# Score maxima in runs of three groups, and an output projection in two dense stretches

## The chip, the cores and the metric

The kernel runs on one core of a Trainium2 chip. The time is in device microseconds (us): the median of three runs of the whole kernel. Five engines work beside each other, each through its own list of instructions in order, and wait for each other by semaphores: TensorE (PE: matmuls; PEld is its weight load), VectorE (DVE), ScalarE (ACT), GpSimd (POOL), and SyncE (SP), which starts the DMA transfers. PE writes into PSUM, eight banks of 128 partitions x 512 float32 numbers. DVE and ACT read PSUM; in this kernel POOL works on SBUF only.

## The reference

One encoder layer over 4096 tokens and 16 meta tokens of width 1024. Per token it is (cut to what matters):

```python
u = rmsnorm(h, norm_g)
f_in, f_gate, q, k, v, a_gate = split(u @ w_in)
f_out = fourier_branch(f_in, w_fmix, b_fmix) * silu(f_gate)     # 512 columns
q, k = rope(rmsnorm(q, q_g)), rope(rmsnorm(k, k_g))             # 8 q heads, 2 kv heads, dim 64
p = softmax(q @ k.T * 64 ** -0.5)                               # over all 4112 keys
a_out = (p @ v) * silu(a_gate)                                  # 512 columns
h = h + concat(f_out, a_out) @ w_out                            # output projection
return rmsnorm(h, final_g)[:, 16:]
```

## The kernel before

Phase A projects the tokens and writes q, k, v and the gates to DRAM. Phase B, which the change is in, does the Fourier branch, the attention, the output projection and the last norm. The Fourier work is finished within the first four pairs; what follows after them is attention with an output projection beside it.

Attention goes in 32 *pairs* `i` = (query block `b` of 512 queries, `p` of four pairs of heads). A pair has 66 *steps* `j`: two heads, 33 tiles of 128 keys each. In a step, PE multiplies one key tile with 512 queries (two matmuls, L1101 and L1102, into a score bank `s`: QK below), ACT takes the exponential (L1105, `pe`), DVE or POOL subtracts its bfloat16 half to get a float16 rest `rr` (L1107; the set `on_dve` says which steps go to DVE), and PE multiplies both with the values into the accumulator `o` (nine small matmuls: PV below). PV runs five steps behind QK (`LAG`).

A softmax needs the maximum of each query's scores. It is found one pair ahead: 32 *groups* a pair (4 query tiles x 8 chunks of 512 keys). A group is two matmuls of 64 rows (L1032), one for each head, which sit in the two halves of the PE array and run beside each other, into the two banks of a tile `m`, and then a DVE reduce of 1024 numbers a partition (L1034). The list `AT` has 16 steps, after whose QK two groups are done. I call such a place a *window*. At the end of the pair `red` (j 61), `fin` (63) and `put` (64) turn the maxima into a row of `qB` for the next pair.

From pair 4 on, pair `i` also does the output projection of one 128-token tile of the block before (`out_units`, L1197): 48 matmuls of 512 columns, 24 for each half of the 1024 output columns, into the one bank `po`. They stand one a step, at steps 15 to 38 and 39 to 62; at the end of each half DVE adds the residual (`hh`, L1202). `mf_parts` and `out_tr` split the Fourier and attention parts of that tile into two float16 halves, which a DMA transposes. The norm of the tile (`out_end`) follows in the next pair at the steps of `NORM`: one square of 1024 columns on ACT (L1214), a few tiny DVE instructions, and a scaling (L1228).

PSUM before: two tiles `m` of two banks (pool `pm`), two score banks (`pq`), `o` and `po`. Nothing but the order of the Python code sets the order on each engine: `top.enter_context(tc.manual_schedule())`. Buffers of a pool are taken in turn, and an instruction that writes one waits for the last reader of what was in it. After pair 31 a tail projects the last block.

Of the kernel before, what the change touches and what calls it, by code (L numbers as in the profile page):

```python
# [738 lines left out]

def phase_b(tc, a, pool, mm3, id32, id16, sc):  # L740
# [10 lines left out]
    with ExitStack() as st:  # L751
# [5 lines left out]
        pm = pool(st, "pm", 2, PSUM)  # L757
        pq = pool(st, "pq", 2, PSUM)
        pv = pool(st, "pv", 1, PSUM)
        pp = pool(st, "po", 1, PSUM)  # L760
# [66 lines left out]
        def dft_units(i, spare):  # L827
# [12 lines left out]
            def one(x, slot, chunk, w, first, last):  # L840
                if not ps:
                    ps.append((pv if spare else pp).tile([P, 512], F32, tag="o" if spare else "po", name="pd"))
# [37 lines left out]
        def trans(u, early):  # L880
            n, sk = (64, stk8) if seq[u] is LAST else (P, stk)
            if early:
                ps = pq.tile([P, 512], F32, tag="s", name="s").rearrange("p (g c)->p g c", c=P)
            else:
                ps = pm.tile([P, 2, 512], F32, tag="m", name="m")[:, 0].rearrange("p (g c)->p g c", c=P)
# [40 lines left out]
        def mix(u, early):  # L926
            n = 64 if seq[u] is LAST else P
            mo = mos[:, 2 * (u % 2):2 * (u % 2) + 2]
            if early:
                t = [pq.tile([P, 512], F32, tag="s", name="s") for _ in range(2)]  # L930
# [92 lines left out]
        def max_units(i):  # L1023
# [4 lines left out]
            def grp(s, c):  # L1028
                t = pm.tile([P, 2, 512], F32, tag="m", name="m")
                for e in range(2):  # L1030
                    rs = slice(64 * e, 64 * e + 64)
                    T.matmul(t[:, e], q[rs, p, s * P:(s + 1) * P], K[kv][rs, 0, c * 512:(c + 1) * 512],  # L1032
                             start=True, stop=True)
                V.tensor_reduce(mx[:, s, :, c], t, axis=AX.X, op=ALU.max)  # L1034

            def meta():
# [4 lines left out]
                t = pm.tile([P, 2, 512], F32, tag="m", name="m")  # L1041
# [19 lines left out]
            def fin():  # L1061

                t = pm.tile([P, 2, 512], F32, tag="m", name="m")
                T.matmul(t[:, 0, :P], n, id16, start=True, stop=True)
                rowt.append(t)
# [11 lines left out]
            return [(lambda s=s, c=c: grp(s, c)) for s, c in order], [meta] if first else [], red, fin, put  # L1077
# [18 lines left out]
        def step(h, kv, t, qa, qb, acc, ob, gate):  # L1096
            d = {}

            def qk(eng):
                s = pq.tile([P, 512], F32, tag="s", name="s")  # L1100
# [49 lines left out]
        def mf_parts(b, s):  # L1150
            mf = mfs.pop((b, s))
            hl = ld["sh1"].tile([P, 2, 512], F16, tag="mh", name="hl")

            def high():
                S.activation(hl[:, 0], mf, AF.Copy)

            def low():
                V.tensor_tensor(out=hl[:, 1], in0=mf, in1=hl[:, 0], op=ALU.subtract)

            def turn():  # L1160
                mt = w1.tile([P, 8, P], F16, tag="mt", name="mt")
                dma_t(mt, hl.rearrange("p w c->p (w c)"))
                mts[b, s] = [mt]

            def turn_last():
                dma_t(hv[:, 8 * s:8 * s + 4], hl[:, 0])
                dma_t(lv[:, 8 * s:8 * s + 4], hl[:, 1])

            return high, low, turn_last if b + 1 == NQB else turn

# [4 lines left out]
        def out_tr(b, s):  # L1175
            src = obs[b][:, s]
            hl = ld["sh1"].tile([P, 2, 512], F16, tag="ml", name="ah")
            S.activation(hl[:, 0], src, AF.Copy)

            def low():  # L1180
                V.tensor_tensor(out=hl[:, 1], in0=src, in1=hl[:, 0], op=ALU.subtract)
                at = w1.tile([P, 8, P], F16, tag="at", name="at")
                dma_t(at, hl.rearrange("p w c->p (w c)"))
                mts[b, s].append(at)

            return low

        def out_units(b, s):
# [3 lines left out]
            def one(k, j):  # L1192
                if j == 0:
                    d["po"] = pp.tile([P, 512], F32, tag="po", name="po")
                cs = slice(k * 512, (k + 1) * 512)
                i, w = j // 3, j % 3
                T.matmul(d["po"], mts[b, s][i // 4][:, i % 4 + (4 if w == 2 else 0)],  # L1197
# [9 lines left out]
        def out_end(b, s, d):  # L1207

            xr, hh = pst.pop((b, s)), d["hh"]
            ss = sm.tile([P, 1], F32, tag="ss", name="ss")  # L1210
            rf = sm.tile([P, 1], F32, tag="rf", name="rf")

            def square():
                S.activation(xr, hh, AF.Square, accum_out=ss)  # L1214

            t = sm.tile([P, 1], F32, tag="r1t", name="r1t")
            h = sm.tile([P, 1], F32, tag="r1h", name="r1h")

            def guess():
                V.tensor_scalar(out=ss, in0=ss, scalar1=1.0 / D, scalar2=EPS, op0=ALU.mult, op1=ALU.add)  # L1220
                root0(rf, ss, t, h)
# [4 lines left out]
            def scale():  # L1226
                yo = w1.tile([P, D], F32, tag="yo", name="yo")
                V.scalar_tensor_tensor(out=yo, in0=hh, scalar=rf, in1=fgb[0], op0=ALU.mult, op1=ALU.mult)  # L1228
                t0 = b * QB + s * P
                dma(a["out"][t0:t0 + P], yo)  # L1230

            return square, guess, newton, newton, newton, scale
# [18 lines left out]
        MT, TR, O0, O1 = 60, 12, 15, 39  # L1251
        NORM = [9, 13, 17, 21, 28, 32]
# [4 lines left out]
        gs += meta  # L1257
        n = 0
        INIT = 11
        while gs:  # L1260
            gs.pop(0)()
            catch_up()
            if gs:
                gs.pop(0)()
# [37 lines left out]
        prev = None  # L1302
        for i, (b, p) in enumerate(pairs):
            if p == 1 and b + 1 < NQB:
                qload(b + 1)
            if i > 4:
                load_xr(b - 1, p)
            elif i == 4:
                load_mf(0, 0)
            ready = {}  # L1310
# [265 lines left out]
```

## Time and profile before

| | |
|---|---|
| median of 3 runs | 3201.99 us (3200.11 to 3205.67) |
| profiled execution | 3203.48 us, its span 3201.7 us, granted PE clock 0.995 |
| busy over the span | PE 98 %, DVE 74 %, POOL 72 %, ACT 52 % |
| 1500 to 2500 us, of 100 us | DVE 79.4 to 81.9, POOL 76.8 to 83.0, ACT 56.0 to 59.7 |
| pairs 4 to 30 | 27 pairs, 72.7 to 73.4 us each |

Busy PE says little here: the record of a 512-column matmul is 379 ns long, and the next one starts 215 ns after it. What PE really does is read from starts: how far one step's first QK matmul lies behind that of the step before. The timeline gives them.

### The profile page before, as it was taken

Reading aid. Unit: us, or ns where it says so; the run is one execution under the profiler, and the core shown is the slowest. Engines: PE = TensorE matmul, PEld = TensorE weight load, DVE = VectorE, ACT = ScalarE, POOL = GpSimd, SP = SyncE. Lnnn points to the kernel's source line nnn. Section 1 sums busy time; section 2 is a strip of 40 time slices with the busy share of each in tenths; the row PEclk is TensorE's granted clock in tenths of the full one; section 3 lists DMA queues with packets and bytes.
Section 4 is the critical chain, followed back from the end, with each engine's and each line's share of the span. In section 5 each row is a group of like instructions: output and inputs, shape, how many; then the busy total and the mean of one; then the engine's idle time right before and its main releaser. Section 6 shows DMA issues by size and latency. Waiting matters only on the chain.

```text
span 3201.7 us, 77151 instructions
## 1 busy us (share of the span) xinstructions
PE 3146.1 (98%) x32291; PEld 1831.4 (57%) x32291; DVE 2373.2 (74%) x3241; ACT 1667.2 (52%) x2965; POOL 2304.3 (72%) x2174
## 2 busy tenths in 40 slices
PE   8999999998999999999999999999999999999998
PEld 4555555545666655555555555555555555555554
DVE  6666566647677778878888778788887887788774
ACT  5433333324555555555555555555555555555563
POOL 5655565536777788877877888887787778888762
PEclk9999999999999999999999999999999999999999
DMA  7444544648422221012111211201120111111112
GB/s 243 146 161 147 152 156 153 182 155 228 131 68 86 78 61 31 28 28 64 28 28 38 54 28 31 58 28 28 38 54 28 35 41 43 31 31 28 28 49 68
DMA packets 238832, 247.67 MB, mean 77 GB/s; under 512 B 134658, under 2 KB 182658, under 8 KB 235538
## 3 DMA queue, kind: packets, MB, share of 16 engines
q1 hardware_dynamic: 224658, 217.57, 23.6%
q10 hardware_dynamic: 13824, 25.17, 2.1%
q8 instruction: 252, 4.13, 0.5%
q14 instruction: 98, 0.80, 0.1%
HBM read 139.59 MB, written 66.38 MB: 64 GB/s over the span
## 4 chain that ended last, share of the span: by engine, by line
PE 74%; DVE 1%; ACT 0%; DMA 0%; issue 0%; POOL 0%; SPq 0%; ACTq 0%; DVEq 0%; POOLq 0%
PE s L1102 14%; PE s L1101 14%; PE o L1122 13%; PE po L1197 9%; PE m L1032 8%; PE o L1129 8%; PE o L1127 2%; PE o L1125 2%; PE pd L849 2%; PE m L1389 1%; DMA acs<-acs_d 0%; ACT pe L1105 0%; POOL rr L1107 0%; DVE rr L1107 0%; DVE thl L893 0%
## 5 line engine op out<-in xcount | busy, mean ns | idle before, releaser
L1107 POOL TENSOR_TENSOR rr<-pe 128x512 f16<-128x512 f32 x1572 | 1709.9, 1105 | 469.9 <-ACT pe L1105 463.4
L1105 ACT ACTIVATE pe<-s 128x512 f32<-128x512 f32 x2112 | 1259.5, 597 | 1016.1 <-PE s L1102 903.2
L1034 DVE TENSOR_REDUCE mx<-m 128x2 f32<-128x1024 f32 x1024 | 1205.9, 1220 | 180.7 <-PE m L1032 179.2
L1129 PE MATMUL o<-VV,rr 128*128 128x65 f16 x8448 | 975.7, 193 | 0.2 <-POOL rr L1107 0.2
L1129 PEld LDWEIGHTS <-rr 128*128 128x128 f16 x8448 | 784.5, 98 | 175.6 <-POOL rr L1107 7.4
L1122 PE MATMUL o<-VV,pe 128*128 128x129 f16 x6336 | 843.3, 222 | 0.8 <-ACT tt L1133 0.8
L1102 PE MATMUL s<-qB,K 128*128 128x512 f16 x2112 | 800.3, 379 | 1.4 <-DVE qB L1069 1.4
L1101 PE MATMUL s<-qA,K 128*128 128x512 f16 x2112 | 799.6, 379 | 0.7 <-ACT pe L1105 0.7
L1122 PEld LDWEIGHTS <-pe 128*128 128x128 bf16 x6336 | 591.1, 97 | 365.1 <-issue 191.0
L1107 DVE TENSOR_TENSOR rr<-pe 128x512 f16<-128x512 f32 x540 | 453.4, 840 | 213.8 <-ACT pe L1105 207.1
L1125 PE MATMUL o<-VV,pe 128*128 128x65 f16 x2112 | 411.5, 195 | 0.0
L1127 PE MATMUL o<-VV,pe 128*128 128x64 f16 x2112 | 410.6, 194 | 0.0
L303 PE MATMUL ps<-wh,xh 128*128 128x512 f16 (+2 forms) x1032 | 352.7, 354 | 9.5 <-ACT xh L291 9.0
L304 PE MATMUL ps<-wl,xh 128*128 128x512 f16 (+2 forms) x1032 | 352.6, 354 | 2.5 <-DVE wl L274 2.5
L1032 PE MATMUL m<-K,qP 64*128 64x512 f16 x2048 | 313.7, 382 | 9.6 <-DMA qP<-qA 6.0
L306 PE MATMUL ps<-wh,xl 128*128 128x512 f16 x768 | 291.6, 380 | 0.0
L1127 PEld LDWEIGHTS <-pe 128*128 128x128 bf16 x2112 | 209.2, 99 | 0.0
L1125 PEld LDWEIGHTS <-pe 128*128 128x128 bf16 x2112 | 206.5, 98 | 0.0
L1102 PEld LDWEIGHTS <-K 128*128 128x128 f16 x2112 | 205.1, 97 | 1.7 <-issue 1.6
L1101 PEld LDWEIGHTS <-K 128*128 128x128 f16 x2112 | 203.4, 96 | 0.9 <-issue 0.4
L1032 PEld LDWEIGHTS <-qP 64*128 64x128 f16 x2048 | 59.7, 94 | 229.2 <-issue 221.3
L1197 PE MATMUL po<-woh,mt 128*128 128x512 f16 x448 | 169.8, 379 | 1.0 <-DVE hh L1202 1.0
(209 smaller groups left out, 3429.2 us busy)
## 6 DMA issues: line engine op xcount, KB each, us to landing
room<-x SPq DMA_DIRECT2D x32, 512.0 KB
xt<-xt SPq DMA_DIRECT2D x32, 512.0 KB
sg<-fx SPq DMA_DIRECT2D x16, 1024.0 KB
xr<-x SPq DMA_DIRECT2D x32, 512.0 KB
out<-yo SPq DMA_DIRECT2D x32, 512.0 KB
ct<-cdo SPq DMA_DIRECT2D x9, 1088.0 KB
fg_d<-g ACTq DMA_DIRECT2D x32, 256.0 KB
ag_d<-g ACTq DMA_DIRECT2D x32, 256.0 KB
```

Source lines behind the costliest of these rows:

```text
L303: T.matmul(o, xh[:, d, :n], wh[:, d, c0:c1], start=d == 0, stop=False)
L1032: T.matmul(t[:, e], q[rs, p, s * P:(s + 1) * P], K[kv][rs, 0, c * 512:(c + 1) * 512], start=True, stop=True)
L1034: V.tensor_reduce(mx[:, s, :, c], t, axis=AX.X, op=ALU.max)
L1101: T.matmul(s, K[kv][:, 0, t * P:(t + 1) * P], qa, start=True, stop=False)
L1102: T.matmul(s, K[kv][:, 1, t * P:(t + 1) * P], qb, start=False, stop=True)
L1105: S.activation(pe, s, AF.Exp, scale=HD ** -0.5)
L1107: eng.tensor_tensor(out=rr, in0=pe, in1=hi, op=ALU.subtract)
L1122: T.matmul(o[:, c0:c0 + 129], hi[:, cs], va, start=t == 0 and s == 0, stop=t == NT, skip_group_check=True)
L1125: T.matmul(o[:, c0:c0 + 65], hi[:, cs], vh, start=False, stop=t == NT, skip_group_check=True)
L1127: T.matmul(o[:, c0:c0 + 64], hi[:, cs], vl, start=False, stop=t == NT, skip_group_check=True)
L1129: T.matmul(o[:, c0:c0 + 65], rr[:, cs], vh, start=False, stop=t == NT, skip_group_check=True)
L1197: T.matmul(d["po"], mts[b, s][i // 4][:, i % 4 + (4 if w == 2 else 0)], wol[i // 4][:, i % 4, cs] if w == 1 else woh[0][:, i, cs], start=j ...
```

## The change

From pair 4 to pair 30 (`banks.wide`) the 32 groups of maxima stand in 11 windows: ten of three groups, and one of two at step 33. For the third group's two banks, a window borrows a score bank (`s1`) and the bank of the output projection (`s2`, `po` before). These two are separate tiles, so such a group has two DVE reduces of 512 numbers instead of one of 1024. Between windows, the scores alternate between `s0` and `s1`; the step before a window uses half of an `m` tile instead, and the window's own step and the one behind it both use `s0`.

The output projection stands in two stretches: six matmuls a step at steps 18 to 21 and at 24 to 27, between the windows at 17, 23 and 29. Its two `hh` come at steps 21 and 27. On DVE there are 21 subtractions a pair (`WIDE_DVE`) instead of 16, on POOL 45 instead of 50. The norm's square is done in two halves (steps 26 and 57), its tiny instructions and its scaling at 18 to 20 of the next pair. The splits of the mixed halves move to 19 and 25 (for the first tile of a block, the attention part to 9), their DMA transposes to 30 (11). In the last pair, the norm is finished inside the pair (58 to 62) instead of behind it. All tiles in PSUM are now named ones, taken by the class `Banks`; pairs 0 to 3 take them in the old order.

```diff
+class Banks:
+
+    AT = {j: 2 if j == 33 else 3 for j in (0, 5, 11, 17, 23, 29, 33, 38, 44, 50, 56)}
+
+    OUT = (18, 24)
...
+        for j, k in zip(self.AT, [*self.AT][1:] + [66]):
+            self.seq.update({(j + x + 1) % 66: 2 if x == k - j - 2 else 0 if x == k - j - 1 else x % 2
+                             for x in range(k - j)})
...
+    def window(self, j):
+        return ([self.single[1:]] if self.wide and self.AT[j] == 3 else []) + [self.pair(), self.pair()]
+
+    def score(self, j=None):
+        if self.wide and j is not None:
+            x = self.seq[j]
+            return self.double[1 - self.m][:, 0] if x == 2 else self.single[x]
+        self.s ^= 1
+        return self.single[self.s]
+
+    def out(self):
+        return self.single[2]
...
-            def grp(s, c):
-                t = pm.tile([P, 2, 512], F32, tag="m", name="m")
+            def grp(s, c, t):
                 for e in range(2):
                     rs = slice(64 * e, 64 * e + 64)
-                    T.matmul(t[:, e], q[rs, p, s * P:(s + 1) * P], K[kv][rs, 0, c * 512:(c + 1) * 512],
-                             start=True, stop=True)
-                V.tensor_reduce(mx[:, s, :, c], t, axis=AX.X, op=ALU.max)
+                    T.matmul(t[e] if isinstance(t, list) else t[:, e], q[rs, p, s * P:(s + 1) * P],
+                             K[kv][rs, 0, c * 512:(c + 1) * 512], start=True, stop=True)
+                if isinstance(t, list):
+                    for e in range(2):
+                        V.tensor_reduce(mx[:, s, e, c:c + 1], t[e], axis=AX.X, op=ALU.max)
+                else:
+                    V.tensor_reduce(mx[:, s, :, c], t, axis=AX.X, op=ALU.max)
...
-            def square():
-                S.activation(xr, hh, AF.Square, accum_out=ss)
+            def square(k):
+                cs = slice(k * 512, (k + 1) * 512)
+                S.activation(pst[b, s][:, cs], d["hh"][:, cs], AF.Square, accum_out=ss[:, k:k + 1])
...
-        MT, TR, O0, O1 = 60, 12, 15, 39
-        NORM = [9, 13, 17, 21, 28, 32]
+        MT = 60
+        NORM = [18, 18, 19, 19, 20]
+        WIDE_DVE = {2, 3, 8, 9, 14, 15, 20, 21, 25, 26, 27, 35, 36, 41, 42, 47, 48, 53, 54, 59, 65}
...
+            banks.wide = i >= 4 and not end
+            at = banks.AT if banks.wide else AT
...
+                for k, o in enumerate(banks.OUT):
+                    for x in range(24):
+                        plan(o + x // 6, halves[k][x])
+                norm = out_end(b - 1, p, d)
+                for j, f in zip(NORM, rest or ()):
+                    plan(j, f)
+                plan(26, norm[0])
+                plan(57, norm[1])
+                rest = norm[2:]
...
+            for j, (qk, pvm) in enumerate(stream(i)):
+                qk(V if j in on_dve else G, j)
+                for f, args in todo.get(j, ()):
+                    f(*args)
+                if j in at and not end:
+                    for t in banks.window(j):
+                        gs.pop(0)(t)
```

Three places where the order changes. The first is on PE, in pair 16, at the window nearest to step 17. Before, this is step 15: QK (L1101, L1102), one matmul of the output projection, four matmuls of maxima (two groups), then the first of PV (L1122):

```order
L1102 MATMUL s_29846<-qB0_7271,K0_6186 128x512
L1197 LDWEIGHTS mt_29282
L1197 MATMUL po_29853<-woh_13619,mt_29282 128x512
L1032 LDWEIGHTS qP0_7273
L1032 MATMUL m_29855<-K0_6186,qP0_7273 128x512
...
L1032 MATMUL m_29859<-K0_6186,qP0_7273 128x512
L1122 LDWEIGHTS pe_29760
```

With the change, steps 17 and 18 (QK is L1137 and L1138, maxima L1064, PV L1158 to L1165, the projection L1221):

```order
L1138 MATMUL s0_7263<-qB0_7270,K0_6186 128x512
...
L1064 MATMUL s1_7264<-K0_6186,qP0_7272 128x512
L1064 LDWEIGHTS qP0_7272
L1064 MATMUL s2_7265<-K0_6186,qP0_7272 128x512
L1064 LDWEIGHTS qP0_7272
L1064 MATMUL m0_7261<-K0_6186,qP0_7272 128x512
...
L1064 MATMUL m1_7262<-K0_6186,qP0_7272 128x512
L1158 LDWEIGHTS pe_28234
...
L1138 MATMUL s0_7263<-qB0_7270,K0_6186 128x512
L1221 LDWEIGHTS mt_27366
L1221 MATMUL s2_7265<-woh_13148,mt_27366 128x512
```

The window has six matmuls now, and the bank `s2` that its second one writes is the bank that the projection's first matmul writes one PV and one QK later.

The second place is PE between the windows at 29 and 33 of the same pair: the first `m` tile that the window at 29 fills, and step 32, whose scores go into half of it:

```order
L1064 MATMUL s2_7265<-K0_6186,qP0_7272 128x512
L1064 LDWEIGHTS qP0_7272
L1064 MATMUL m0_7261<-K0_6186,qP0_7272 128x512
...
L1158 LDWEIGHTS pe_28546
...
L1137 MATMUL m0_7261<-qA0_7268,K0_6186 128x512
```

Steps 30 and 31 (scores in `s0` and `s1`) lie between; before, a score never went into an `m` tile.

The third place is DVE from the window at 17 to that at 23 (L1068 and L1070 are reduces, L1143 a subtraction, L1262 to L1271 the norm, L1253 its scaling, L1199 a split, L1226 `hh`):

```order
L1068 TENSOR_REDUCE mx_27998<-s1_7264 128x1
L1068 TENSOR_REDUCE mx_27998<-s2_7265 128x1
L1070 TENSOR_REDUCE mx_27998<-m0_7261 128x2
L1070 TENSOR_REDUCE mx_27998<-m1_7262 128x2
L1243 TENSOR_SCALAR ss2_26762<-ss2_26762 128x1
...
L1143 TENSOR_TENSOR rr_28392<-pe_28391 128x512
L1253 SCALAR_TENSOR_TENSOR yo_28401<-hh_27183,rf_26763,fgb_13146 128x1024
L1199 TENSOR_TENSOR hl_28378<-mf_28238,hl_28378 128x512
L1143 TENSOR_TENSOR rr_28417<-pe_28416 128x512
L1226 SCALAR_TENSOR_TENSOR hh_28426<-s2_7265,xr_28050 128x512
L1068 TENSOR_REDUCE mx_27998<-s1_7264 128x1
```

Before, the same engine had two reduces and one subtraction at each window, and the norm's pieces spread between them:

```order
L1034 TENSOR_REDUCE mx_29559<-m_30015 128x2
L1107 TENSOR_TENSOR rr_30049<-pe_30048 128x512
L1034 TENSOR_REDUCE mx_29559<-m_30070 128x2
L1034 TENSOR_REDUCE mx_29559<-m_30074 128x2
L1107 TENSOR_TENSOR rr_30108<-pe_30107 128x512
L1244 TENSOR_SCALAR r1t_29495<-rf_29494,r1h_29496 128x1
```

The order on DVE is now four reduces in a row, then two subtractions, and only in the projection's stretches the rest.

More of the change, by code (lines that the diff above doesn't have):

```diff
@@ L756, in phase_b @@
         sm = pool(st, "bs", 2)
-        pm = pool(st, "pm", 2, PSUM)
-        pq = pool(st, "pq", 2, PSUM)
+        pm = pool(st, "pm", 1, PSUM)
         pv = pool(st, "pv", 1, PSUM)
-        pp = pool(st, "po", 1, PSUM)
+        banks = Banks([pm.tile([P, 2, 512], F32, name=f"m{i}") for i in range(2)],
+                      [pm.tile([P, 512], F32, name=f"s{i}") for i in range(3)])
         K = [ld["kk"][0], bp.tile([P, 2, (NT + 1) * P], F16, name="K1")]
@@ L841, in one @@
                 if not ps:
-                    ps.append((pv if spare else pp).tile([P, 512], F32, tag="o" if spare else "po", name="pd"))
+                    ps.append(pv.tile([P, 512], F32, tag="o", name="pd") if spare else banks.out())
                 cs = slice(0, NC_) if x == 0 else slice(NC_, 512)
@@ L929, in mix @@
             if early:
-                t = [pq.tile([P, 512], F32, tag="s", name="s") for _ in range(2)]
+                t = [banks.score() for _ in range(2)]
             else:
-                t = pm.tile([P, 2, 512], F32, tag="m", name="m")
+                t = banks.pair()
                 t = [t[:, i] for i in range(2)]
@@ L1040, in meta @@
                     met[b] = sm.tile([P, 2, 4, 4], F32, tag="met", name="met")
-                t = pm.tile([P, 2, 512], F32, tag="m", name="m")
+                t = banks.pair()
                 for x in ps:
@@ L1061, in fin @@
             def fin():
-                t = pm.tile([P, 2, 512], F32, tag="m", name="m")
+                t = banks.pair()
                 T.matmul(t[:, 0, :P], n, id16, start=True, stop=True)
@@ L1076, in max_units @@
             first = p == 0 or (b == 0 and p == 2)
-            return [(lambda s=s, c=c: grp(s, c)) for s, c in order], [meta] if first else [], red, fin, put
+            return [(lambda t, s=s, c=c: grp(s, c, t)) for s, c in order], [meta] if first else [], red, fin, put
         obs = {}
@@ L1097, in step, with qk @@
             d = {}
-            def qk(eng):
-                s = pq.tile([P, 512], F32, tag="s", name="s")
+            def qk(eng, j):
+                s = banks.score(j)
                 T.matmul(s, K[kv][:, 0, t * P:(t + 1) * P], qa, start=True, stop=False)
@@ L1193, in one @@
                 if j == 0:
-                    d["po"] = pp.tile([P, 512], F32, tag="po", name="po")
+                    d["po"] = banks.out()
                 cs = slice(k * 512, (k + 1) * 512)
                 i, w = j // 3, j % 3
-                T.matmul(d["po"], mts[b, s][i // 4][:, i % 4 + (4 if w == 2 else 0)],
+                T.matmul(d["po"], mts[b, s, i // 4][:, i % 4 + (4 if w == 2 else 0)],
                          wol[i // 4][:, i % 4, cs] if w == 1 else woh[0][:, i, cs], start=j == 0, stop=j == 23)
@@ L1256, in phase_b @@
         gs, meta, red, fin, put = max_units(0)
-        gs += meta
+        gs += [lambda t: meta[0]()] if meta else []
         n = 0
@@ L1366, in phase_b @@
                     pend.pop(0)()
+            assert not gs
+        banks.wide = False
         b = NQB - 1
@@ L1371, in tail_tr @@
             src = obs[b][:, s]
-            t = pq.tile([P, 512], F32, tag="s", name="s")
+            t = banks.score()
             for j in range(4):
@@ L1383, in tail_mm @@
             if part == 0:
-                accs[s] = pm.tile([P, 2, 512], F32, tag="m", name="m")
+                accs[s] = banks.pair()
             for k in range(2):
```

169 lines of the change are left out of this document (76 added, 93 removed).

## The prediction

> **What bounds the kernel now.** I read the busy shares first, then the pair's length, then PE's timeline step by step, then what DVE, ACT and POOL do behind a window. The page's shares and two groups of its fifth part:
>
> ```profile
> PE 3146.1 (98%) x32291; PEld 1831.4 (57%) x32291; DVE 2373.2 (74%) x3241; ACT 1667.2 (52%) x2965; POOL 2304.3 (72%) x2174
> ...
> L1107 POOL TENSOR_TENSOR rr<-pe 128x512 f16<-128x512 f32 x1572 | 1709.9, 1105 | 469.9 <-ACT pe L1105 463.4
> ...
> L1034 DVE TENSOR_REDUCE mx<-m 128x2 f32<-128x1024 f32 x1024 | 1205.9, 1220 | 180.7 <-PE m L1032 179.2
> ...
> L1107 DVE TENSOR_TENSOR rr<-pe 128x512 f16<-128x512 f32 x540 | 453.4, 840 | 213.8 <-ACT pe L1105 207.1
> ```
>
> PE is never idle in the records, and DVE and POOL sit idle before 0.2 to 0.5 ms of their work because ACT or PE isn't there yet. So PE's own stream is the limit. The changed part's length comes from `put`, once a pair, by the view of line 1069 from 1200 to 3150 us:
>
> ```profile
> L1069 DVE TENSOR_TENSOR qB<-m,id x26: 1222/1222/1222, 1257.4 to 3080.0; 8x1024 f16<-8x1024 f32 x26
> ```
>
> 25 pairs in 1822.6 us: 72.9 us a pair, and 27 pairs change (4 to 30). PE's timeline in one of them shows a plain step, one with a window, one with only a projection matmul:
>
> ```profile
> 2000.72 0.38 PE L1101 MATMUL s<-qA,K 128*128 128x512 f16 x1
> 2000.94 0.38 PE L1102 MATMUL s<-qB,K 128*128 128x512 f16 x1
> 2001.15 0.22 PE L1122 MATMUL o<-VV,pe 128*128 128x129 f16 x1
> ...
> 2001.51 0.38 PE L1101 MATMUL s<-qA,K 128*128 128x512 f16 x1
> ...
> 2002.43 0.38 PE L1101 MATMUL s<-qA,K 128*128 128x512 f16 x1
> 2002.65 0.38 PE L1102 MATMUL s<-qB,K 128*128 128x512 f16 x1
> 2002.86 0.38 PE L1197 MATMUL po<-woh,mt 128*128 128x512 f16 x1
> 2003.17 0.60 PE L1032 MATMUL m<-K,qP 64*128 64x512 f16 x4
> 2003.71 0.23 PE L1122 MATMUL o<-VV,pe 128*128 128x129 f16 x1
> ...
> 2004.08 0.38 PE L1101 MATMUL s<-qA,K 128*128 128x512 f16 x1
> ...
> 2005.08 0.38 PE L1101 MATMUL s<-qA,K 128*128 128x512 f16 x1
> ```
>
> A plain step is 0.79 us (2000.72 to 2001.51): QK 0.43 (two matmuls 0.215 apart), PV 0.36. A projection matmul adds 0.215 (2004.08 to 2005.08 is 1.00). The window step takes 1.65, so two groups add 0.65. Four matmuls of 0.215, two at a time, are 0.43 of it. The rest lies at the edges: L1032 starts 0.31 behind L1197 and not 0.215 (0.095 at entry), and L1122 0.54 behind L1032 and not 0.43 (0.11 at exit). **A window costs 0.205 us beside its matmuls**, whatever it holds. Little else is lost: the step from 2001.51 to 2002.43 is 0.13 too long, a `rr` that came late from POOL, and such lateness, which PE meets between windows 5 and 15, I count as 0.2 us a pair.
>
> **The change part by part.** *Windows.* 16 become 11, with the same 64 matmuls: 5 x 0.205 = 1.03 us a pair off PE, if nothing waits. *The projection* has its 48 matmuls of 0.215 as before; its place costs PE nothing by itself. What decides is whether banks are free in time, and that hangs on DVE. I put the step of a window at 0: QK to 0.43, entry to 0.525, three groups of 0.215 to 1.17, exit to 1.28, PV to 1.64, next QK. For DVE these rows (timeline of DVE, three places, and one of ACT):
>
> ```profile
> 2003.61 2.36 DVE L1034 TENSOR_REDUCE mx<-m 128x2 f32<-128x1024 f32 x2 [0.49 <-PE m L1032]
> 2006.40 0.69 DVE L1107 TENSOR_TENSOR rr<-pe 128x512 f16<-128x512 f32 x1 [0.43 <-ACT pe L1105]
> 2007.00 0.27 DVE L1244 TENSOR_SCALAR r1t<-rf,r1h 128x1 f32<-128x1 f32 x1
> ...
> 2030.20 0.69 DVE L1202 SCALAR_TENSOR_TENSOR hh<-po,xr 128x512 f32<-128x512 f32 x1
> 2030.81 2.35 DVE L1034 TENSOR_REDUCE mx<-m 128x2 f32<-128x1024 f32 x2
> ...
> 2003.06 0.60 ACT L1105 ACTIVATE pe<-s 128x512 f32<-128x512 f32 x1 [0.26 <-PE s L1102]
> ```
>
> A reduce starts 0.44 behind the start of its matmuls (2003.17 to 2003.61). An instruction of 512 numbers out of PSUM takes 0.69 and lets the next start 0.61 after it (2030.20 to 2030.81); two reduces of 1024 take 2.36, so they start 1.14 apart. Reduces of one bank of 512 are not in this stretch of the trace in that form; the nearest is the meta tokens' reduce, by the groups of 1500 to 2500 us:
>
> ```profile
> L1050 DVE TENSOR_REDUCE met<-m 128x32 f32<-128x512 f32 x3 | 2.1, 692 | 1.5 <-PE m L1047 1.5
> ```
>
> So with DVE free, the four reduces of a window start at 0.97 (`s1`), 1.58 (`s2`), 2.19 (`m0`) and 3.33 (`m1`), end at 1.66, 2.27, 3.41 and 4.55, and DVE is free again at 4.49. PE goes on about 0.05 after DVE's end, by the chain of waits in the last pair:
>
> ```profile
> 3120.11 0.70 DVE hh L1202
> 3120.82 0.04 issue
> 3120.86 0.38 PE po L1197
> ```
>
> Now who comes too early. `s1` is wanted by the QK two steps on, at 1.64 + 0.79 = 2.43: free since 1.66. `m0`, six steps on, at 4.8: free. But **`s2` is wanted by the projection at 2.07** (step 18 behind the window at 17, step 24 behind that at 23) and is free at 2.27 + 0.05: **0.25 us of waiting, twice**. And at step 32, only three steps behind the window at 29, the score goes into `m0` at 1.64 + 2 x 0.79 = 3.22, free at 3.46: **0.24 us**. The window at 33 then waits a further 0.04 for the exponential of 32. Behind each wait stand PE's next PV and QK, so it all counts. If DVE comes to the window at 17 late, that adds in full. From 11 to 17 DVE has 4.49 - 0.97 = 3.52 of reduces and two subtractions. The view of line 1107 from 1260 to 3080 us has these as
>
> ```profile
> L1107 POOL TENSOR_TENSOR rr<-pe x1249: 1029/1039/1802, 1259.1 to 3079.7; 128x512 f16<-128x512 f32 x179
> L1107 DVE TENSOR_TENSOR rr<-pe x400: 679/693/1602, 1259.6 to 3074.0; 128x512 f16<-128x512 f32 x134
> ```
>
> that is 0.69 mostly, 0.84 in the mean, at most 1.6. 3.52 + 2 x 0.76 (0.84 less the overlap of 0.08) = 5.04, in 1.64 + 5 x 0.79 = 5.59 us. DVE keeps up, with half a microsecond to spare; I take 0.05 for the cases where it doesn't. Bounds: 0, and 0.4, if both subtractions in front of 17 cost 1.1.
>
> *The stretch 17 to 23* has the norm too. Its price from the tail's copy of the same chain:
>
> ```profile
> 3149.55 0.12 DVE L1220 TENSOR_SCALAR ss<-ss 128x1 f32<-128x1 f32 x1
> ...
> 3151.83 1.28 DVE L1228 SCALAR_TENSOR_TENSOR yo<-hh,rf,fgb 128x1024 f32<-128x1024 f32 x1
> ```
>
> 2.28 for ten small ones, about 2.45 for the eleven now: DVE is through at 4.49 + 2.45 = 6.94, does `rr` of step 20 at 7.3, the scaling to 9.1, a split to 9.7, `rr` of 21 to 10.3, and `hh` to 11.0. PE's four steps are 0.79 + 6 x 0.215 = 2.08 each, so the window at 23 starts at 1.64 + 0.25 + 8.32 + 0.79 = 11.0 and writes `s2` at 11.5. Half a microsecond to spare; if it is gone, the price is what `hh` is late, up to 0.5 a pair.
>
> *ACT.* An exponential starts 0.41 behind L1102 (2002.65 to 2003.06), so ends about 1.23 behind its step's start. Step and window before a reused bank leave 1.57 or 1.64: covered, by 0.3. The first `m` group of a window wants the score of the step before at 0.74 + 0.79 = 1.53: covered. The square was one insertion of 1.14 us (its row in the chain of the last pair is the first below); a half lies in a long step (26), the other at 57, where 0.6 fits in the slack of two steps. Nothing for both; uncovered, 0.1 to 0.3.
>
> ```profile
> 3090.56 1.14 ACT xr L1214 x2
> ```
>
> *POOL* loses 5 x 1.04 to 1.11 us a pair, and three subtractions in front of each window is less than the four to five it has between steps 0 and 15 now. I let half of PE's 0.2 us of lateness go: 0.1. *SP* issues the same DMAs, some at other places. The shortest way is the attention part at a block's first tile: its transpose goes out at step 11, behind it on SP stands only the load of `mf`, and PE wants it at 20, about 10 us later by the steps above. In the waits of SP the `mf` load, which needs the transpose to have landed, waited for it twice:
>
> ```profile
> SPq L1148 <- DMA at<-ah: 2.8, 2, 1.7
> ```
>
> That is hidden; 10 us late would be a stop of PE in 7 of the 27 pairs. *Last pair:* the second `hh` wait (the rows at 3120) and the square's stall go, the norm at 58 to 62 puts some 3.7 us on DVE between subtractions: -0.5 in all, +-1.
>
> **Sum.** A pair: -1.03 - 0.1 + 0.25 + 0.25 + 0.24 + 0.04 + 0.05 = -0.30 us. 27 x 0.30 = 8.1, and 0.5: **8.6 us off 3203.48, 3194.9**. The profiled execution lies 1.5 above the median of the runs, so **3193** for the median, 0.28 % faster. About 0.2 % (6.4 us) is what a measurement of this kernel can tell from no change.
>
> **Rivals.**
>
> *The waits on DVE don't appear* (DVE answers a single bank's group sooner than 0.44, or its reduce is shorter). For it: 0.44 is for a tile of two banks. Against: two thirds of the wait is the two reduces in a row. All 1.13 stays: 27 x 1.13 + 0.5 = 31: 3171.
>
> *They eat the rest up.* If subtractions in front of 17 and 23 run 0.3 late on top, a pair gains nothing: 3201. For it: the maximum of 1.6 in the row above; against: the median of 0.69.
>
> *The 0.205 goes with the groups, not with the window.* Then three groups lose 0.31, nothing is saved, and only the waits stay: 27 x 0.73 - 0.5 = +19: 3221, slower. For it: the trace has only windows of two in these pairs. Against: the two gaps stand at entry and exit, and inside, four matmuls take what two pairs need. The Trainium skill (TensorEngine Tiling (Array Packing), Key Properties) says that a change of tiling mode drains the engine, which is a price for each change and speaks against this rival.
>
> *DVE and POOL hold each other up* in the tight part, steps 30 to 65. PE needs 36 x 0.79 + 0.65 + 4 x (0.645 + 0.205) = 32.5 us there. POOL has 26 subtractions and one head's end:
>
> ```profile
> 2030.67 0.53 POOL L1137 TENSOR_TENSOR ob<-tt 128x192 f32<-128x192 f32 x1
> ...
> 2032.20 0.61 POOL L1140 TENSOR_TENSOR ob<-ob,rc 128x256 f32<-128x256 f32 x1
> ```
>
> 27.0 at 1.04, and 2.1: 29.1. If none of DVE's ten subtractions (6.9) could run beside POOL's, they would need 36.0: 3.5 late. PV may be 4.35 behind QK's start and needs its `rr` 2.35 behind it, so 2 us are forgiven: 1.5 a pair, less the 0.30: 27 x 1.2 = +32: 3234, slower. It decides once POOL's mean is above (32.5 - 2.1 + 2)/26 = 1.25; it is 1.105 now. The Trainium skill (SBUF — State Buffer, Who interferes with whom) has just such a rule: VectorE's second SBUF input comes through ports that GpSimd shares, and the later one waits until the other is done. By that rule this rival would be the forecast; the medians of 0.69 and 1.04 in the rows of line 1107 say that most don't wait.
>
> **How the numbers follow.** Forecast 0.48 (own range 3186 to 3200), no waits 0.20, eaten up 0.15, by groups 0.07, held up 0.10. Faster by over 0.2 % (below 3195.6): two thirds of the first, and the second: 0.53. Within: the rest of the first but a little, most of the third: 0.26. Slower: 0.21. The range leaves out the fourth's and second's outer halves and the last: 3172 to 3222.
>
> **What would show it.** Right: a window step of 1.64 us on PE with six maxima; steps 18 and 24 of 2.3 us against 2.08 at 19 and 25, step 32 late by 0.24, and pairs of 72.6. Wrong: subtractions on DVE above 1.0 in the mean, steps without window above 0.79 between 36 and 65 (held up), window steps of 1.75 (by groups), or steps 18 and 24 at 2.08 (no waits).

## The result, and the profile after

The changed kernel takes **3232.8 us** (median of 4 runs, 3230.4 to 3235.6), and the kernel before 3202.7 beside it: a ratio of 1.0094, with a 95 % interval of 1.0077 to 1.0111. It is slower by 0.94 %. The forecast was 3193, and the range ended at 3222: direction and range were both wrong. Its profiled execution took 3233.05 us, with a span of 3231.2 and a granted clock of 0.995 as before, so the clock is not the reason.

The page's shares, its chain of waits by engine and line, and four groups of its fifth part:

```profile
PE 3142.7 (97%) x32291; PEld 1861.5 (58%) x32291; DVE 2535.5 (78%) x3674; ACT 1673.4 (52%) x3021; POOL 2187.8 (68%) x2039
...
PE 56%; DVE 18%; issue 1%; DMA 1%; ACT 1%; POOL 0%; SPq 0%; ACTq 0%; DVEq 0%; POOLq 0%
...
L1143 POOL TENSOR_TENSOR rr<-pe 128x512 f16<-128x512 f32 x1437 | 1583.5, 1126 | 615.9 <-ACT pe L1141 609.7
...
L1070 DVE TENSOR_REDUCE mx<-m 128x2 f32<-128x1024 f32 x754 | 884.9, 1214 | 76.9 <-PE m L1064 76.5
...
L1143 DVE TENSOR_TENSOR rr<-pe 128x512 f16<-128x512 f32 x675 | 615.4, 930 | 191.2 <-ACT pe L1141 187.7
...
L1068 DVE TENSOR_REDUCE mx<-s 128x1 f32<-128x512 f32 x540 | 344.7, 678 | 60.0 <-PE s L1064 57.2
```

The row of the same chain before was

```profile
PE 74%; DVE 1%; ACT 0%; DMA 0%; issue 0%; POOL 0%; SPq 0%; ACTq 0%; DVEq 0%; POOLq 0%
```

DVE's share of the chain went from 1 % to 18 %. By the shares, PE is busy for 98 % before and 97 % now, so they don't show it. DVE's reduces cost what they were thought to (678 ns for a single bank, 1214 for a pair). Its subtraction does not: 930 ns in the mean, against 840 before, while the mean of POOL's rose from 1105 to 1126.

PE's waits from 1260 to 3050 us (us in total, times, longest) name what comes too late:

```profile
PE s L1137 <- DVE mx L1068: 18.0, 36, 1.6
PE s L1221 <- DVE mx L1068: 6.2, 18, 0.5
PE o L1165 <- POOL rr L1143: 1.9, 7, 0.3
```

In the kernel before, the same view has no row at all. L1068 are the reduces of the two single banks that a window borrows, L1137 the scores that want such a bank back, L1221 the projection. The third row, PV waiting for a subtraction of POOL's, is small. The view leaves out waits under 0.15 us.

**Where the time came from, step by step.** From the starts of the first QK matmul in PE's timeline, the length of every step, as a mean over the 27 changed pairs. The last column is the mean above what the same step takes undisturbed (0.785 us, 1.65 with a window of three, 1.43 with a window of two and no projection, 2.08 with six projection matmuls):

| steps | predicted, us a pair | measured, us a pair |
|---|---|---|
| five windows fewer | -1.03 | -1.03 |
| late `rr` from POOL, nearly all at step 14 | -0.10 | -0.11 |
| 18 (bank `s2`, and DVE late) | +0.30 | +0.42 |
| 24 (`s2`) | +0.25 | +0.21 |
| 31 to 33 (`m0`, then the exponential) | +0.28 | +0.22 |
| 6 (behind the window at 5) | 0 | +0.35 |
| 11 and 12 (behind the window at 11) | 0 | +0.77 |
| 1 and 3 (in the first pair of a block only) | 0 | +0.09 |
| 59 (the second square) | 0 | +0.08 |
| sum | -0.30 | +1.00 |

72.90 became 73.89 us a pair, 26.9 us in 27 pairs. The tail is in the row of `put`, here of the kernel before (all 32 of them) and of the changed one:

```profile
L1069 DVE TENSOR_TENSOR qB<-m,id x32: 1222/1222/1222, 782.2 to 3080.0; 8x1024 f16<-8x1024 f32 x32
```

```profile
L1105 DVE TENSOR_TENSOR qB<-m,id x32: 1222/1222/1223, 781.1 to 3107.9; 8x1024 f16<-8x1024 f32 x32
```

Behind the last `put`, the last pair and the tail take 3201.7 - 3080.0 = 121.7 us before and 3231.2 - 3107.9 = 123.3 now: +1.6, where -0.5 was predicted. The span grew by 29.5, so 1.0 of it lies in front of pair 4. The first `put` stands between 777.9 and 785.1 us in the changed kernel and its nine variants below, whose code up to it is the same. That 1.0 is not put down to anything.

**The place.** The chain of waits of the changed kernel from 3036 to 3056 us, the front of one pair in order of time:

```profile
3036.84 0.77 DVE rr L1143
...
3037.64 1.29 DVE mx L1068 x2
3038.93 2.26 DVE mx L1070 x2
3041.19 2.07 DVE rr L1143 x2
3043.26 0.09 DVE rc L1171
3043.35 1.18 DVE mx L1068 x2
3044.53 2.26 DVE mx L1070 x2
3046.79 2.46 DVE rr L1143 x2
3049.25 1.20 DVE mx L1068 x2
3050.45 1.60 DVE mx L1070 x2
...
3052.64 1.66 DVE rr L1143 x2
3054.30 1.21 DVE mx L1068 x2
```

From the subtraction of step 65 (3036.84) to the window at 17, the chain is DVE's alone: the four reduces of the window at 0, two subtractions, the four reduces of the window at 5, two subtractions, and so on. Two subtractions in a row take 2.07 in front of the window at 5, 2.46 in front of 11, and 1.66 in front of 17. The prediction had them at 2 x 0.76 = 1.52.

In another such pair, the timelines of PE, DVE and POOL show one wait from end to end:

```profile
2087.20 0.39 PE L1064 MATMUL s<-K,qP 64*128 64x512 f16 x2
...
2088.32 0.38 PE L1137 MATMUL s<-qA,K 128*128 128x512 f16 x1
...
2089.46 0.38 PE L1137 MATMUL s<-qA,K 128*128 128x512 f16 x1 [0.20 <-DVE mx L1068]
```

```profile
2084.01 2.34 DVE L1070 TENSOR_REDUCE mx<-m 128x2 f32<-128x1024 f32 x2
2086.27 2.54 DVE L1143 TENSOR_TENSOR rr<-pe 128x512 f16<-128x512 f32 x2
2088.74 1.27 DVE L1068 TENSOR_REDUCE mx<-s 128x1 f32<-128x512 f32 x2
```

```profile
2084.78 7.93 POOL L1143 TENSOR_TENSOR rr<-pe 128x512 f16<-128x512 f32 x7
```

The window at 11 begins at 2087.20. DVE is in its subtractions until 2088.7, and its first reduce is through at about 2089.42 (2088.74 + 0.68). PE's score for step 13 wants that bank and starts at 2089.46. Step 12 is 1.14 long instead of 0.785. During all of this POOL is in a run of seven subtractions without a gap.

### The profile page after: what moved, and what is told of

It reads as the page before. It is cut to its first block, busy times and chain, and to the rows that moved or that the text cites. A ratio compares the mean times of both kernels' runs of the same rounds, so it can differ in the third digit from the quotient of the medians.

```text
span 3231.2 us, 77836 instructions
## 1 busy us (share of the span) xinstructions
PE 3142.7 (97%) x32291; PEld 1861.5 (58%) x32291; DVE 2535.5 (78%) x3674; ACT 1673.4 (52%) x3021; POOL 2187.8 (68%) x2039
## 4 chain that ended last, share of the span: by engine, by line
PE 56%; DVE 18%; issue 1%; DMA 1%; ACT 1%; POOL 0%; SPq 0%; ACTq 0%; DVEq 0%; POOLq 0%
PE s L1221 9%; PE s L1137 9%; PE s L1138 9%; PE o L1158 8%; PE o L1165 6%; DVE mx L1070 6%; DVE mx L1068 6%; DVE rr L1143 5%; PE m L1064 3%; PE s L882 2%; PE s L1064 2%; PE m L1137 2%; PE m L1138 2%; PE o L1163 1%; PE o L1161 1%; PE m L1423 1%
## 5 line engine op out<-in xcount | busy, mean ns | idle before, releaser
L1143 POOL TENSOR_TENSOR rr<-pe 128x512 f16<-128x512 f32 x1437 | 1583.5, 1126 | 615.9 <-ACT pe L1141 609.7
L1141 ACT ACTIVATE pe<-s 128x512 f32<-128x512 f32 x1815 | 1081.2, 598 | 908.7 <-PE s L1138 858.6
L1165 PE MATMUL o<-VV,rr 128*128 128x65 f16 x8448 | 975.8, 193 | 3.6 <-POOL rr L1143 1.9
L1070 DVE TENSOR_REDUCE mx<-m 128x2 f32<-128x1024 f32 x754 | 884.9, 1214 | 76.9 <-PE m L1064 76.5
L1165 PEld LDWEIGHTS <-rr 128*128 128x128 f16 x8448 | 784.2, 98 | 194.0 <-POOL rr L1143 7.6
L1158 PE MATMUL o<-VV,pe 128*128 128x129 f16 x6336 | 840.7, 221 | 0.9 <-ACT tt L1169 0.9
L1158 PEld LDWEIGHTS <-pe 128*128 128x128 bf16 x6336 | 593.8, 97 | 322.7 <-issue 132.0
L1143 DVE TENSOR_TENSOR rr<-pe 128x512 f16<-128x512 f32 x675 | 615.4, 930 | 191.2 <-ACT pe L1141 187.7
L1137 PE MATMUL s<-qA,K 128*128 128x512 f16 x1815 | 687.6, 379 | 21.4 <-DVE mx L1068 20.1
L1138 PE MATMUL s<-qB,K 128*128 128x512 f16 x1815 | 688.1, 379 | 1.4 <-DVE qB L1105 1.4
L1068 DVE TENSOR_REDUCE mx<-s 128x1 f32<-128x512 f32 x540 | 344.7, 678 | 60.0 <-PE s L1064 57.2
L1141 ACT ACTIVATE pe<-m 128x512 f32<-128x512 f32 x297 | 177.3, 597 | 127.9 <-PE m L1138 114.7
L1064 PE MATMUL m<-K,qP 64*128 64x512 f16 x1508 | 229.9, 379 | 10.0 <-DMA qP<-qA 6.0
L1138 PEld LDWEIGHTS <-K 128*128 128x128 f16 x2112 | 205.0, 97 | 31.8 <-issue 27.3
L1137 PEld LDWEIGHTS <-K 128*128 128x128 f16 x2112 | 203.5, 96 | 1.8 <-issue 1.7
```

The costliest lines, as they stand in the source:

```text
L1064: T.matmul(t[e] if isinstance(t, list) else t[:, e], q[rs, p, s * P:(s + 1) * P], K[kv][rs, 0, c * 512:(c + 1) * 512], start=True, stop=True)
L1068: V.tensor_reduce(mx[:, s, e, c:c + 1], t[e], axis=AX.X, op=ALU.max)
L1137: T.matmul(s, K[kv][:, 0, t * P:(t + 1) * P], qa, start=True, stop=False)
L1138: T.matmul(s, K[kv][:, 1, t * P:(t + 1) * P], qb, start=False, stop=True)
L1141: S.activation(pe, s, AF.Exp, scale=HD ** -0.5)
L1143: eng.tensor_tensor(out=rr, in0=pe, in1=hi, op=ALU.subtract)
```

## The experiments

The theory after the result had two parts. *A*: DVE's subtractions are held up while POOL reads SBUF at the same time, so DVE comes late to the windows at 5 and 11 (and a little at 17). *B*: the shared bank `s2`, and `m0` at step 32, are wanted too soon, as predicted. The rivals were that the dense stretch costs something by itself, and that DVE is late because of how its work is ordered, whatever POOL does.

**Dense stretches with windows of two**

```diff
-            banks.wide = i >= 4 and not end
+            banks.wide = False
```

(16 windows of two groups and 16 subtractions on DVE as before; the projection stays dense.)

> The windows of three are undone (16 windows of two groups at the old steps, old set of subtractions on DVE, scores alternate between two banks); the two dense stretches of the projection, the halved square and the moved norm and splits stay. Theory (DVE comes late to the windows of three, and the lent banks are waited for): nothing of that is left, the 5 x 0.205 us of windows come back, PE waits for POOL less than before; 3194 to 3206 us. Rival (the dense stretches themselves cost, by the norm and both hh crowded into them): most of the loss stays, 3220 us or more, with steps 18 to 27 longer than 2.08 plus a window's 0.645.

Measured: 3226.0, ratio 1.0071 (1.0056 to 1.0086). My theory fell here, and the rival had the size, but not the place: half of the change alone is slower, too, and yet the dense steps are 2.08, as they should be. What is too long is step 55 by 0.44 and step 52 by 0.14, where windows stand three steps apart, and step 11 by 0.19, where PV waits for POOL's `rr`. DVE's timeline around steps 49 to 55:

```profile
2124.75 1.25 DVE L1143 TENSOR_TENSOR rr<-pe 128x512 f16<-128x512 f32 x1
2125.93 2.34 DVE L1070 TENSOR_REDUCE mx<-m 128x2 f32<-128x1024 f32 x2
2128.20 1.25 DVE L1143 TENSOR_TENSOR rr<-pe 128x512 f16<-128x512 f32 x1
2129.37 2.34 DVE L1070 TENSOR_REDUCE mx<-m 128x2 f32<-128x1024 f32 x2
```

3.44 us for a window's reduces and one subtraction (2125.93 to 2129.37), without a gap. PE's three steps and a window are 3 x 0.785 + 0.645 = 3.0 now that no projection matmul stands in each of them; with it, they were 3.65. POOL stands in a run of twelve subtractions without a gap there (2117.53 to 2131.41). By an estimate from the 0.64 measured below, the same work of DVE would have taken 2.27 + 0.64 = 2.9 without POOL's reading, so this loss too may be part A; no run here tests it.

**Subtractions moved out of the front**

```diff
-        WIDE_DVE = {2, 3, 8, 9, 14, 15, 20, 21, 25, 26, 27, 35, ...
+        WIDE_DVE = {2, 8, 14, 19, 20, 21, 24, 25, 26, 27, 28, 35, ...
```

> Changed kernel with the subtractions of steps 3, 9 and 15 given to POOL and those of 19, 24 and 28 to DVE: as many on each engine, but DVE has one and not two in front of the windows at 5, 11 and 17. Theory: DVE is on time at these three windows, the waits at steps 6 and 12 (0.45 and 0.36 us) go and that at 18 falls from 0.42 to 0.25, and the first pair of a block, 1.8 us longer than it should be, loses most of that; -1.0 us a pair, 3203 to 3212 us. Rival (POOL can't take them there: it has a head's end of 2 to 2.5 us in the same stretch): PV waits for late subtractions on POOL instead, 3225 us or more.

Measured: 3208.05, ratio 1.0011 (1.0001 to 1.0021). 24.7 us of the loss are gone. Steps 6 and 12 are at their undisturbed length, except in the first pair of each block, where step 12 keeps 0.43. Steps 18, 24 and 31 still wait, 0.21, 0.21 and 0.37 (the subtraction of step 28, now on DVE, makes the last one longer). Step 10 is 0.12 too long now, where PV waits for a `rr` of POOL's: the rival, POOL too late in the front, is there in small. This run shows that DVE's lateness in front of 5 and 11 is what costs, not yet that POOL causes it.

**POOL writes zeros, once and twice**

```diff
-                eng.tensor_tensor(out=rr, in0=pe, in1=hi, op=ALU.subtract)
+                if banks.wide and eng is G and j < 18:
+                    G.memset(rr, 0.0)
+                else:
+                    eng.tensor_tensor(out=rr, in0=pe, in1=hi, op=ALU.subtract)
```

> Changed kernel, but POOL's subtractions at steps 0 to 17 of pairs 4 to 30 are left out: POOL fills rr with zeros there, which reads nothing. DVE's program is the same word for word. Theory (DVE's subtractions are slow because POOL reads SBUF at the same time): two subtractions in front of a window take 1.3 us and not 2.1 to 2.5, and the waits at 6 and 12 go, that at 18 falls to 0.25; 3196 to 3210 us. Rival (DVE has too much to do, whatever POOL does): its subtractions stay above 1 us each in this stretch and the waits stay, 3225 to 3235 us.

> As e3_fill, but GpSimd writes its tile with zeros twice, so that it is as long at work (2 x 0.52 us) as it was with the subtraction, and reads nothing; the same part of the computation is left out. Theory (VectorE's subtraction is held up by GpSimd's reading of SBUF): as e3_fill, 3192 to 3202, VectorE's subtractions at a mean of 0.82 to 0.86 us and no loss at steps 6 and 12. Rival (what counts is that GpSimd is at work, by its writes or because its results come later): 3215 to 3235, the subtractions at 0.9 us or more.

(The second has the `memset` line twice.) Measured: 3196.1 with one `memset`, ratio 0.9978 (0.9968 to 0.9987), and 3197.3 with two, 0.9980 (0.9971 to 0.9989). DVE has exactly the subtractions of the changed kernel in both. The timeline of DVE with two, then that of POOL at the same time:

```profile
2065.62 1.28 DVE L1147 TENSOR_TENSOR rr<-pe 128x512 f16<-128x512 f32 x2
...
2070.35 1.35 DVE L1147 TENSOR_TENSOR rr<-pe 128x512 f16<-128x512 f32 x2
2072.13 1.29 DVE L1068 TENSOR_REDUCE mx<-s 128x1 f32<-128x512 f32 x2 [0.44 <-PE s L1064]
```

```profile
2069.90 0.53 POOL L1144 MEMSET rr<- 128x512 f16 x1
2070.49 0.53 POOL L1145 MEMSET rr<- 128x512 f16 x1
2070.95 0.53 POOL L1144 MEMSET rr<- 128x512 f16 x1
2071.53 0.52 POOL L1145 MEMSET rr<- 128x512 f16 x1
```

In these lines POOL is at work with no more than 0.06 us between two instructions, as in the changed kernel, but only writes. Two subtractions on DVE then take 1.28 and 1.35, not 2.15 and 2.54 as in the timeline of the changed kernel at the same two places, and DVE waits 0.44 us for the next window. With one `memset`, POOL is idle beside the first two but for the last 0.27 us, and they take 1.28 as well. So it is POOL's subtractions, which read, that hold DVE up, not that POOL is busy or late: part A is shown, the ordering rival is out. The Trainium skill (SBUF — State Buffer, Who interferes with whom) says that a VectorE instruction with two SBUF inputs contends with a GpSimd instruction that reads SBUF and not with one that only writes it, and that a reduce never contends. The runs agree on each of these points: the reduce's mean is 1214 or 1215 ns in all three kernels.

With one `memset`, what is left above the undisturbed lengths is 0.21 at step 18, 0.21 at 24, 0.20 at 31, 0.08 at 59, and 0.09 at 1 and 3. The first three are the prediction's own waits. A pair is 0.32 shorter than before, where 0.30 was predicted; that it comes so close is in part luck, since the predicted waits came out 0.19 smaller and 0.17 came that wasn't in the sum. The median of 3196 lies 3 above the forecast 3193.

**The banks in another order**

```diff
-        return ([self.single[1:]] if self.wide and self.AT[j] == 3 else []) + [self.pair(), self.pair()]
+        one = self.single[1:] if j not in (17, 23) else self.single[:0:-1]
+        return ([one] if self.wide and self.AT[j] == 3 else []) + [self.pair(), self.pair()]
...
+            if j == 32:
+                return self.single[2]
```

(The windows at 17 and 23 fill `s2` first and `s1` second, and step 32's score goes into `s2`.)

> Changed kernel with two banks changed and no work moved: at the windows of 17 and 23 the lent group fills the projection's bank first and the score bank second, so that its reduce comes first; and step 32 puts its score into the projection's bank, idle by then, and not into half of a double tile. Theory: the wait at 18 falls from 0.42 to none or 0.1, those at 24 and 32 (0.21 each) go, those at 6 and 12 stay; -0.7 us a pair, 3211 to 3217 us. Rival (the waits only move to the next reduce that is late): 3228 to 3233 us.

Measured: 3210.7, ratio 1.0025 (1.0014 to 1.0035): 22.1 us less than the changed kernel. The waits at 18, 24 and 31 are gone, and those at 6 and 12 stay as they were. Part B holds, at a little more than was expected of it.

**Both, and a finer version.** The fifth kernel has the edits of "Subtractions moved out of the front" and of "The banks in another order" together. The sixth adds these:

```diff
-                plan(57, norm[1])
+                plan(41, norm[1])
...
-                        plan(58 + j, f)
+                        plan(44 + j, f)
...
-                    plan(j + 1, low)
+                    plan(j + (4 if j == 9 else 1), low)
```

(and the transpose at 14 and the load at 15 in a block's first pair, and step 28's subtraction back on POOL).

> The changed kernel with both edits: VectorE's subtractions of steps 3, 9 and 15 given to GpSimd and those of 19, 24 and 28 taken from it, and the third score bank filled first in the windows at 17 and 23, with step 32's score in it. Theory (two separate losses, each paid at its own steps: VectorE late behind the windows at 5 and 11, and the shared bank at steps 18, 24 and 32): the two gains add, 3232.8 - 24.7 - 22.1 = 3186, so 3182 to 3193, below the kernel before. Rival (both edits use the same slack of TensorE, so that the second brings little once the first is made): 3200 to 3208.

> As the run before with four more edits: the subtraction of step 28 back on GpSimd; in the first pair of each block the low half of the attention split at step 13 and its transpose at 14 (10 and 11 before), with the load of the next rows at 15 (12 before); the second square at step 41 (57 before); the last pair's norm at steps 44 to 48 (58 to 62 before). Theory: step 31 loses its 0.16 us (27 times, 4 us), the first pairs some 0.5 to 0.9 us (7 times, 3 to 6 us), step 59 its 0.07 us (2 us) and the flush of the last pair 2 us: 7 to 14 us below the run before, 3172 to 3184. Rival (the transpose that starts three steps later lands after the projection asks for it at step 20, or the square at 41 makes a score bank late there): no better than the run before, 3185 or more.

Measured: 3185.1, ratio 0.9939 (0.9927 to 0.9952), and 3181.05, ratio 0.9928 (0.9914 to 0.9941). The two gains add up to within a microsecond (3186 expected): A and B are separate losses. **Both versions beat the kernel before and the changed one**; 3181 is 0.72 % faster than before. The second step was worth 4 us and not the 7 to 14 expected, and the intervals of the two overlap, so the traces have to say it. Of PE's waits from 1260 to 3050 us, this is all that the view has of the sixth kernel, and below it its `put`:

```profile
PE s L1067 <- DVE hh L1229: 1.0, 6, 0.2
```

```profile
L1108 DVE TENSOR_TENSOR qB<-m,id x32: 1222/1223/1223, 779.0 to 3056.8; 8x1024 f16<-8x1024 f32 x32
```

Steps 12 and 59 are undisturbed now. Step 31 was so in the fifth kernel already, by its bank, so the 4 us expected from it could not come. The tail is 3179.3 - 3056.8 = 122.5, against 3183.3 - 3060.3 = 123.0 in the fifth: 0.5, where 2 were expected. The projection's `hh` in the first pairs is new among the waits (step 23, 0.23, in six of the seven), and step 10 keeps its 0.12 from POOL. Steps 18 to 22 and 24 to 27 are within 0.02 us of undisturbed in the sixth kernel, so with windows of three the dense stretch costs nothing by itself.

**The split in a block's first pair, alone**

The `low` line above, with its transpose and load, in the changed kernel.

> The changed kernel with one edit, in the first pair of each block alone (7 of the 27 pairs): the low half of the attention split at step 13 and its transpose at 14 instead of 10 and 11, the load of the next rows at 15 instead of 12. Theory (these pairs are 1.83 us longer than the others because this subtraction stands in front of the window at 11 on VectorE): steps 6 and 12 of these pairs come down to what they are in the others, 7 x 1.5 = 10 us less in all, 3219 to 3226. Rival (the length of these pairs has another cause, the first tiles of a block or the transpose): 3230 to 3236.

Measured: 3233.1, no change. The theory fell, but not in favour of the rival as I had put it. Step 12 of a block's first pair, 2.55 long in the changed kernel, is 1.11 now. Step 18 of the same pair, 2.29 there, is now 3.95. PE and DVE in such a pair:

```profile
2314.23 0.38 PE L1137 MATMUL s<-qA,K 128*128 128x512 f16 x1
...
2316.53 0.38 PE L1221 MATMUL s<-woh,mt 128*128 128x512 f16 x1 [1.71 <-DVE mx L1068]
```

```profile
2312.18 1.06 DVE L1199 TENSOR_TENSOR hl<-ob,hl 128x512 f16<-128x512 f32 x1
2313.16 2.12 DVE L1143 TENSOR_TENSOR rr<-pe 128x512 f16<-128x512 f32 x2
2315.21 1.27 DVE L1068 TENSOR_REDUCE mx<-s 128x1 f32<-128x512 f32 x2
```

The split stands in front of the window at 17 instead of the one at 11, and the loss moved with it: 1.44 us left step 12, 1.66 came to step 18. DVE has no slack in that stretch, and at both places tried the split cost 1.4 to 1.7 us (its own record is 1.52 in the changed kernel). In the finer version, where DVE has three subtractions fewer in that stretch and `s2` is filled first, the same move leaves step 12 at 0.79 and 18 at no more than 2.14.

**Windows of two, spread differently**

```diff
+        EVEN = [0, 5, 9, 14, 18, 20, 22, 24, 26, 28, 30, 34, 39, 44, 49, 54]
...
-            at = banks.AT if banks.wide else AT
+            at = AT if i < 4 else EVEN
```

(`banks.wide` is False again, and a subtraction goes to DVE two steps behind each window, as before.)

> As e1_dense (sixteen windows of two groups in every pair, the projection in two dense stretches), but in the pairs from the fifth on the windows stand at steps 0, 5, 9, 14, 18, 20, 22, 24, 26, 28, 30, 34, 39, 44, 49 and 54: seven of them in the dense steps, and at least four steps apart elsewhere. Theory (e1_dense lost because its windows stand three steps apart where no projection paces TensorE any longer; the dense stretch itself costs nothing): the late windows' 0.6 us a pair goes, 3200 to 3210, as the kernel before. Rival (the dense stretch itself costs, by steps of 0.785 us in which GpSimd and VectorE can't keep up wherever the windows stand): 3216 or more.

Measured: 3323.0, ratio 1.0372 (1.0354 to 1.0389), far outside of both. PE's waits from 1260 to 3150 us, the page's chain, and POOL's timeline over the front of a pair:

```profile
PE m L1064 <- DVE mx L1070: 36.7, 72, 0.7
PE o L1165 <- POOL rr L1143: 22.0, 25, 0.9
PE o L1158 <- ACT tt L1169: 9.5, 24, 0.4
```

```profile
PE 35%; POOL 31%; DVE 7%; issue 2%; ACT 2%; DMA 1%; SPq 0%; ACTq 0%; DVEq 0%; POOLq 0%
```

```profile
2113.18 11.93 POOL L1143 TENSOR_TENSOR rr<-pe 128x512 f16<-128x512 f32 x11
2125.06 0.53 POOL L1173 TENSOR_TENSOR ob<-tt 128x192 f32<-128x192 f32 x1
```

A pair is 4.35 us longer than before, and the loss has three places. Steps 22 and 30 are 0.56 and 1.37 too long: windows stand two steps apart there, and PE waits for an `m` tile that DVE hasn't reduced yet (the first row). Steps 65, 1 to 3, 10 and 11 are 1.83 too long together. There POOL, with its 50 subtractions, sets the pace: steps 1 to 3 are 1.0 long, one POOL subtraction each, and step 10 is 1.88. Step 38 is 0.56 too long, where PV waits for ACT to read the accumulator (the third row). My placing cured DVE's trouble at steps 52 and 55 by making trouble for DVE elsewhere and for POOL. So whether a dense stretch with windows of two could be had for nothing is not settled by this run; it suggests that a window, too, is time in which POOL catches up.

## Why the prediction was wrong

*What failed* is one term, the time that DVE needs between two windows: "3.52 + 2 x 0.76 (...) = 5.04, in 1.64 + 5 x 0.79 = 5.59 us. DVE keeps up, with half a microsecond to spare". The 0.76 came from a view that mixes all steps of the kernel before, in which DVE's subtractions stand one by one. In the changed kernel two subtractions stand in a row while POOL is in a run of its own, unbroken in front of 11 and beginning 0.6 us late in front of 5. They take 2.46 and 2.07, so the sum is 6.0 and 5.6 and not 5.04.

The term was also asked for in the wrong place. The bound, 1.1 each, was put in front of the window at 17 only, as 0.4 a pair (by the same sum, 3.52 + 2.2 is just 0.13 over 5.59), and the windows at 5 and 11 were put at nothing, though the same four reduces and two subtractions stand in front of them. Between the windows at 0 and 5 lie only 1.65 + 4 x 0.785 = 4.79 us, so even 5.04 was 0.25 too much there, and DVE comes to 11 late already. By the prediction's own rows a score forgives 0.72 us of lateness (wanted at 2.43, free at 1.66, and 0.05). At 2087.20, in the lines above, DVE's first reduce is 1.10 later than the 0.44 behind its matmuls (2088.74 and not 2087.64); less the 0.72 that makes 0.38, and 0.36 was measured. (The 0.25 alone would have been forgiven: it was the price that failed.) The table's rows for 6 and for 11 and 12 are this and the block's first pairs (below): +1.12 a pair, 30 of the 38 us between 3195 and 3233. With POOL's reading gone, both rows are gone, and so is 0.21 of the 0.42 at step 18.

*The rival "DVE and POOL hold each other up"* had the mechanism and, by chance, the time: 3234. Of the rule of the Trainium skill that it named (SBUF — State Buffer, Who interferes with whom), the part on which instructions contend holds here, by the runs with `memset`. That the later one waits until the other is done does not: one subtraction of each engine in a row would be 0.64 + 1.04 = 1.68 us, and DVE's took 1.27 beside an unbroken run of POOL's. But the rival stood on steps 30 to 65, where only 31 (its bank), 33 (0.02) and 59 (the second square) are too long, and on POOL's mean reaching 1.25; POOL's went to 1.126 only. It was DVE that paid, in the front. The medians by which I set it aside (0.69, 1.04) say that most instructions of the whole run don't wait, not that those in the tight stretch don't. By the sign that I had named for it, "subtractions on DVE above 1.0 in the mean", the 930 of the profile's page would even have spoken against it: a mean over the run is the wrong sign for six instructions of a pair.

*The block's first pair* was thought hidden: I looked at the transpose's way to step 20 and not at the subtraction of the split in front of the window at 11. It costs these pairs the 1.4 us each that left step 12 when it was moved, 7 x 1.4 = 10 us of the 26.9, and is contained in the table's row for 11 and 12.

*The last pair*: -0.5 was predicted, +1.6 came. Its norm at 58 to 62 stands between subtractions on DVE, as I wrote, and may make them late for the flush of PV, at the very end. Moving it to 44 gave 0.5 back, from the fifth kernel to the sixth; what the rest is has not been looked for.

*What was right.* The price of a window, 0.205 whatever it holds: 2087.20, quoted above, lies in a step of 1.65 with six matmuls of maxima, and five fewer windows save the 1.03. So the rival "goes with the groups" is out. The waits: 0.25 was predicted for step 24 and 0.21 came, 0.24 for step 32 and 0.20 came. Step 18 was 0.42 with DVE late and 0.21 without. "No waits" is out, too. And without POOL's reading in the front, a pair is 0.32 shorter than before, close to the 0.30 of the sum, in part by luck, as said there.

## What to carry to other kernels

Cost an instruction that stands in a tight stretch at its price beside what the other engines do in that stretch, not at its mean over the run. Where VectorE's subtraction ran beside an unbroken run of GpSimd's, that was up to twice the price alone.

When matmuls are gathered from many steps into a few, the other steps get shorter for everybody: ask of each engine whether it can still answer in the shorter step. The two runs with windows of two suggest that the projection's matmul in each step had been part of what let VectorE and GpSimd keep up.

Moving work within a stretch in which an engine has no slack moved the wait and saved nothing (the split); moving it out of the stretch saved most of the wait (the three subtractions, 24.7 us).

## What the runs showed of the hardware

- DVE's subtraction of two SBUF operands of 128x512 takes 0.64 us in a row with POOL all but idle (1.28 for two), 0.64 to 0.68 beside a POOL that only writes (1.28 and 1.35), and 1.27 beside a POOL that reads without a gap (2.54). POOL pays far less: its seven in a row took 7.93, 1.13 each, against the median of 1.04. Even held up, a subtraction is shorter than one of each in a row (1.27 against 0.64 + 1.04 = 1.68), so the two don't simply take turns. How they share isn't shown.
- A POOL that writes all the time (`memset` of 0.53 us, one behind the other) does not slow DVE measurably: the mean of all of DVE's subtractions is 837 ns with two of them and 835 with one, against 930 with POOL reading.
- A window of half-row matmuls between full ones costs PE 0.205 us beside its matmuls, at its entry and its exit, the same within 0.02 for four matmuls in it as for six.
